# A hybrid state-space and attention layer: other gates in the first stage, keys and queries split two heads at a time, and the time steps projected with the values

## The chip, the cores and the metric

The kernel runs on one core of one Trainium2 chip, as one program with one launch. The core has five engines that run their own instruction streams and wait for one another by semaphores: TensorE (PE in the profile, with PEld for its weight loads), VectorE (DVE), ScalarE (ACT), GpSimd (POOL) and SyncE (SP), which here issues the DMAs. Working data lie in SBUF (128 partitions), matmul results in PSUM, eight banks of 512 fp32 numbers for each partition, and everything else in HBM. The metric is the device time of the program in microseconds, the median of several runs.

## The reference

One layer (D_MODEL 1024) over 512 latent tokens with 256 context tokens ahead of them. Both are normed and modulated; a single input projection feeds everything else:

```python
p_lat = h_lat @ w_in            # columns: z 2048, x/B/C 3072, dt 64, q 1024, k 256, v 256, gates 2048
p_ctx = h_ctx @ w_in
# state-space branch (SSD): 32 heads of 64 in 4 groups, both directions, chunks of 128 tokens
dt = softplus(dt_raw + dt_bias);  la = dt * (-exp(a_log))
y_l = ssd_bidir(xs_l, bm_l, cm_l, dt_l, la_l, state_of_the_context)
ssd_lat = rmsnorm((y_l + d_skip * xs_l) * silu(z), ssd_norm_g)
# attention branch: 16 query heads, 4 key/value heads, width 64, rotary,
# keys: the latent tokens within 128 places, all context tokens, and a sink logit
att_lat = window_ctx_attention(rope(q_l), rope(k_l), v_l, k_c, v_c, sink)
# merge
g = sigmoid(p_lat[..., G0:])
o = (g_ssd * (ssd_lat @ w_o_ssd) + g_att * (att_lat @ w_o_att)) @ w_out
x = x + gt1 * o
x = x + gt2 * conv_ffn(modulate(rmsnorm(x), ...))
```

Three column blocks of `w_in` matter here beside q, k and v: `z`, 16 blocks of 128 columns, which gate the state-space output through a silu; the 2048 columns of the two branch gates, 16 blocks `g`, which pass through a sigmoid; and the 64 columns of `dt`, the time steps of 32 heads in two directions.

## The kernel before

**Numbers.** Everything is fp32. Where a product must be precise, each factor is split into a high part, `hi`, stored as fp32r, and the rest, `lo = x - hi`; the product is then three matmuls, hi·hi, hi·lo and lo·hi. `gemm` (L186) does this for eight blocks of 128 rows of depth. A weight block of 128 x 1024 numbers is loaded by SP into `wraw`, cast to `whi` by ACT (L149) and subtracted to `wlo` by DVE (L150). `run` (L167) takes a list of steps, each with the weight blocks that it needs, and issues the load and split of one block ahead.

**Order.** The first stage's matmuls, and those of the last stages, stand in an order written out by hand. Everywhere else a planner orders the instructions of each engine by what they depend on, so that one engine's order in the program need not be that of the source. Buffers come from pools: a temporary named `ta` has 3 buffers, `tb`, `tc` and `te` 2 each (L113), and a new one waits until an old one's readers, DMAs too, are done. All DMAs stand in SP's one stream.

**First stage (to about 70 us).** While the modulation vectors are made from `w_mod` and the input is normed, the first five branch gates (NG = 5, L294) are projected: `products` (L399) adds up in five PSUM banks `pg`. Since the first rows are used before the norm is known, the shift that modulation adds is brought in at the end as a bias `gb` (L443 to L448). Then a tanh goes to HBM as `ts_d` for each gate (L504 to L507); a sigmoid is kept as tanh(x/2), and the consumer adds 1. Then the context is normed into `hch` and `hcl` (L382 to L387).

**Keys, queries, values.** `k_step` (L592) projects two key heads for latents and context; `rope` (L574) rotates them, and `split_k` (L584) writes each head's hi and lo into the upper and the lower 64 partitions of `khi` and `klo`, by eight ACT and eight DVE instructions. `q_split` (L606) puts one query head's hi into one half of a tile and its lo into the other, so that one matmul with `khi` and one with `klo` give hi and lo at once: two ACT casts and two DVE subtractions on 64 partitions per step. `v_step` (L616) projects the values with tokens on the partitions, 256 columns, two token blocks to a bank.

**Attention (about 100 to 320 us).** Four key heads j and four query blocks b: `block(j, b)` (L650) makes the scores of four heads (one buffer of two banks, L663), takes the minimum on DVE (L675), the exponential on ACT (L679), scales, transposes by TensorE (L697), splits (L700, L701) and multiplies by the values (L702, L703). Between blocks stand projections, `q_step(2)` to `q_step(7)`, `k_step(1)`, and twelve filling steps from the list `fill` (L714): a `z_step` (L515) makes tanh(z/2) on ACT, (tanh + 1)·z on DVE into a `te`, and stores it to `zs_d`; a `g_step` (L527) makes a tanh into a `tb` and stores it to `ts_d` or `ta_d`. The list holds z0 to z15 and then g5 to g15.

**Steps' tables (about 320 to 400 us).** Three more fills (z12 to z14), eight output projections of attention (`oa_step`), and `dt_tables` (L753): a gemm of 64 columns for latents and context, then a chain on ACT and DVE: softplus by a series, with a reciprocal (L769), the decays, and twelve scans along the chunks. `cs_d` goes to HBM.

**The scan (about 400 to 760 us).** For each of four groups: six projections with a short convolution, then four chunks of 128 tokens. `chunk_in` (L1006) loads two 512 KB tables `fb` broadcast from `cs_d` and makes the decay matrix E; `chunk_out` (L1041) multiplies with the forward and the backward state into two parts, each in a `te` (L1050), multiplies E with the inputs into a PSUM bank `yd` (L1054), adds up on POOL (L1059 to L1061) and on DVE (L1062). The next group's projections fill the time; the fourth group has no next one, so it takes fills (L1097): z15, g5, g6 and g7 are each one group's first fill, g8 to g13 fill the fourth group. `gate` (L1066) loads `zs_d` and multiplies.

After it come output projection, merge and the feed-forward part, which the change does not touch.

## Time and profile before

| | |
|---|---|
| median of 3 runs | 1292.92 us (1292.82 to 1294.89) |
| profiled execution | 1291.25 us, of which the span is 1289.5 us |
| granted TensorE clock, mean | 0.998 |
| PE busy | 1260.1 us, 98% of the span, 6482 instructions |
| DVE busy | 899.2 us, 70% |
| ACT busy | 664.8 us, 52% |
| POOL busy | 138.6 us, 11% |
| DMA | 168.66 MB, mean 131 GB/s |

Matmuls overlap one another, so a matmul's recorded length (about 390 ns at 512 columns) is longer than the time that it costs (the distance between two starts). The span runs from the first to the last instruction; an instruction's wait is put down to the one that released it.

### The profile page before, as it was taken

What the parts mean: (1) busy time and instruction counts of PE and PEld (TensorE: products, weight loads), DVE (VectorE), ACT (ScalarE), POOL (GpSimd) and SP (SyncE); (2) the same over time, 40 slices, a digit from 0 to 9 for tenths busy, and PEclk for the clock granted to TensorE, in tenths of its full rate; (3) what the DMA queues carried; (4) which work ended last, traced back from release to release, by engine and by line L of the source; (5) the groups of instructions that cost most, each with busy time, mean ns of one, the idle gap of its engine ahead of it and who ended that gap; (6) DMA issues with size and microseconds to landing.
All of it is one profiled execution on the core that took longest, in us unless ns stands there. A gap on an engine that the chain in (4) does not pass through costs nothing.

```text
span 1289.5 us, 17298 instructions
## 1 busy us (share of the span) xinstructions
PE 1260.1 (98%) x6482; PEld 1025.6 (80%) x6482; DVE 899.2 (70%) x1431; ACT 664.8 (52%) x1230; POOL 138.6 (11%) x113
## 2 busy tenths in 40 slices
PE   7999999999999999999999999999999999999997
PEld 4698777887778878788787777888888888888886
DVE  3867888778495588888888757776677767772323
ACT  3568888767434466475673744223544444442221
POOL 0000000000000043433434440000200000000000
PEclk9999999999999999999999999999999999999999
DMA  8621112222345245454445558867133433333331
GB/s 321 255 94 51 42 58 66 66 74 66 99 127 184 82 117 137 139 134 131 137 140 170 165 192 290 252 221 229 33 115 115 131 114 114 115 107 93 92 101 66
DMA packets 86931, 168.66 MB, mean 131 GB/s; under 512 B 6784, under 2 KB 42112, under 8 KB 86848
## 3 DMA queue, kind: packets, MB, share of 16 engines
q1 hardware_dynamic: 86848, 167.56, 41.5%
q8 instruction: 51, 0.84, 0.3%
q14 instruction: 32, 0.26, 0.1%
HBM read 150.62 MB, written 16.91 MB: 130 GB/s over the span
## 4 chain that ended last, share of the span: by engine, by line
PE 84%; DVE 7%; ACT 5%; issue 2%; DMA 1%; POOL 0%; SPq 0%; DVEq 0%; ACTq 0%; POOLq 0%
PE acc L193 21%; PE acc L192 21%; PE acc L195 21%; PE mis L1054 2%; PE mis L1047 2%; PE score L668 2%; PE pt L697 2%; PE mis L404 2%; PE mis L960 1%; PE po L702 1%; DVE wlo L150 1%; PE mis L888 1%; PE mis L978 1%; PE po L703 1%; PE acc L1196 1%
## 5 line engine op out<-in xcount | busy, mean ns | idle before, releaser
L150 DVE TENSOR_TENSOR wlo<-wraw,whi 128x1024 fp32r<-128x1024 f32 x161 | 203.8, 1266 | 133.0 <-ACT whi L149 131.7
L149 ACT CAST whi<-wraw 128x1024 fp32r<-128x1024 f32 x161 | 166.7, 1036 | 220.7 <-PE acc L193 186.6
L192 PE MATMUL acc<-hlh,whi 128*128 128x512 f32 (+1 forms) x496 | 204.1, 412 | 0.1
L193 PE MATMUL acc<-hll,whi 128*128 128x512 f32 (+1 forms) x496 | 196.1, 395 | 0.0
L195 PE MATMUL acc<-hlh,wlo 128*128 128x512 f32 (+1 forms) x496 | 195.4, 394 | 0.2 <-DVE wlo L150 0.2
L192 PE MATMUL acc<-mh,whi 128*128 128x512 f32 x376 | 146.5, 390 | 0.0
L193 PE MATMUL acc<-ml,whi 128*128 128x512 f32 x376 | 146.4, 389 | 0.0
L195 PE MATMUL acc<-mh,wlo 128*128 128x512 f32 x376 | 146.3, 389 | 0.0
L192 PEld LDWEIGHTS acc<-hlh,whi 128*128 128x128 f32 (+1 forms) x496 | 93.0, 187 | 21.3 <-issue 4.1
L193 PEld LDWEIGHTS acc<-hll,whi 128*128 128x128 f32 (+1 forms) x496 | 93.0, 187 | 19.9 <-issue 4.1
L195 PEld LDWEIGHTS acc<-hlh,wlo 128*128 128x128 f32 (+1 forms) x496 | 92.8, 187 | 19.5 <-issue 1.0
L195 PEld LDWEIGHTS acc<-mh,wlo 128*128 128x128 f32 x376 | 70.6, 188 | 14.8
L192 PEld LDWEIGHTS acc<-mh,whi 128*128 128x128 f32 x376 | 70.6, 188 | 14.7
L193 PEld LDWEIGHTS acc<-ml,whi 128*128 128x128 f32 x376 | 70.6, 188 | 14.6 <-DVE ml L1165 0.2
L962 POOL TENSOR_TENSOR st<-st,eT 128x512 f32<-128x512 f32 x24 | 32.8, 1368 | 410.3 <-ACT st L980 396.7
L860 ACT ACTIVATE ta<-acc,half 128x512 f32<-128x512 f32 (+1 forms) x66 | 46.6, 706 | 41.0 <-PE acc L195 41.0
L245 POOL TENSOR_TENSOR rs<-ms,phalf 128x2 f32<-128x2 f32 (+1 forms) x7 | 6.1, 877 | 548.9 <-DVE ms L244 548.9
L675 DVE CUSTOM_DVE_ANT_0 p<-score,winm,nsink 128x512 f32<-128x512 f32 (+1 forms) x64 | 52.0, 812 | 15.0 <-PE score L668 14.2
L192 PE MATMUL acc<-fh,whi 128*128 128x512 f32 x154 | 60.0, 390 | 0.0
L195 PE MATMUL acc<-fh,wlo 128*128 128x512 f32 x154 | 59.9, 389 | 0.0
L193 PE MATMUL acc<-fl,whi 128*128 128x512 f32 x154 | 59.9, 389 | 0.0
L679 ACT ACTIVATE p<-p,mneg 128x512 f32<-128x512 f32 (+1 forms) x64 | 49.7, 777 | 17.2 <-DVE mneg L675 16.9
(320 smaller groups left out, 2818.8 us busy)
## 6 DMA issues: line engine op xcount, KB each, us to landing
wraw<-wup SPq DMA_DIRECT2D x44, 512.0 KB, 3.6
fb<-cs_d SPq DMA_DIRECT2D x32, 512.0 KB, 6.7
wraw<-wm SPq DMA_DIRECT2D x32, 512.0 KB, 3.6
wraw<-wx SPq DMA_DIRECT2D x24, 512.0 KB, 3.6
wm<-wm SPq DMA_DIRECT2D x16, 512.0 KB, 8.1
wraw<-wz SPq DMA_DIRECT2D x16, 512.0 KB, 3.6
wraw<-wos SPq DMA_DIRECT2D x16, 512.0 KB, 4.6
wraw<-wdn SPq DMA_DIRECT2D x16, 512.0 KB, 3.5
```

The source lines that it names most:

```text
L149: S.copy(hi[:, :n], r[:, :n])
L150: V.tensor_tensor(lo[:, :n], r[:, :n], raw(hi[:, :n]), ALU.subtract)
L192: T.matmul(ps, wh, xh[:, k0 + k, :], start=a, stop=False)
L193: T.matmul(ps, wh, xl[:, k0 + k, :], start=False, stop=False)
L195: T.matmul(ps, wl, xh[:, k0 + k, :], start=False, stop=b)
L404: T.matmul(pg[i], w[a][:, i * P : (i + 1) * P], h[b], start=st and a + b == 0, stop=en and a == 1, skip_group_check=True,)
L668: T.matmul(ps[:, o : o + w], Q[h][:, b * P : (b + 1) * P], k[:, j, z[0] * P : z[0] * P + w], start=v == 0 and o % 512 in (0, P), stop=v == ...
L675: V.tensor_tensor_reduce(p[:, :n], ps[:, o0 : o0 + n], m, op0=ALU.add, op1=ALU.min, scale=1.0, scalar=nsink[:, h : h + 1], accum_out=mn,)
L679: S.activation(p[:, :n], p[:, :n], AF.Exp, bias=mn, scale=-1.0, accum_out=den[:, i : i + 1])
L697: T.transpose(pt[:, i * P : (i + 1) * P], pts[i][:, c * P : (c + 1) * P], ident)
L860: S.activation(o[:, :n], ps[:, :n], AF.Identity, scale=hcol(base_w, stride + i), bias=hcol(base_b, i))
L962: G.tensor_tensor(h8(n), h8(s), bc64(eT[:, z0 : z0 + 8, c]), ALU.mult)
```

## The change

Four things change.

First, the five blocks projected in the first stage are z0 to z4 and no longer g0 to g4. Each now needs a tanh, the value itself with its bias (an Identity on ACT, into a `ta`), a product on DVE, and a store to `zs_d`; the bias is kept twice, halved and whole. The fills follow: attention's twelve are g0 to g2, z5 and g3 to g10; before the steps' tables stand z6 to z8; the groups' first fills are z9, z10, z11 and z12; the fourth group's are z13, z14, z15, g11, g12 and g13.

Second, `q_split` and `split_k` work on 128 partitions, two heads at once: one ACT cast and one DVE subtraction. The halves are then put in their places by DMAs between SBUF tiles, three for a query step and six for a key step (`double_k`).

Third, the steps' 64 columns are appended to the values' 256, so that `v_step` has matmuls of 320 columns, one bank for each of six token blocks. The steps are copied to a `te`, transposed by six TensorE instructions placed in q2's gemm (`steps_turn`, `with_turn`), and stored to `dt_d`.

Fourth, `dt_tables` has no gemm and reads `dt_d`.

```diff
-    src["dt", 0] = wdt, 512
+    for i, n in enumerate((3, 3, 2)):
+        src["v", i] = wv[i, :, : n * 320], n * 320
...
     for i in range(2):
         src["k", i] = wk[i], 1024
-        src["v", i] = wv[i], 1024
...
+    dt_d = dpool.tile([64, L + LC], F32, name="dt_d")
...
-        gb = cpool.tile([P, 8], F32, name="gb")
+        gb = cpool.tile([P, 16], F32, name="gb")
...
-                S.activation(gb[:, v : v + 2 * n - 1 : 2], pbias[:, 256 + 3 * v : 256 + 3 * v + n], AF.Copy, scale=0.5)
+                for c, f in ((0, 0.5), (8, 1.0)):
+                    S.activation(
+                        gb[:, c + v : c + v + 2 * n - 1 : 2], pbias[:, 256 + 3 * v : 256 + 3 * v + n], AF.Copy, scale=f
+                    )
...
             S.activation(t, pg[i], AF.Tanh, scale=0.5, bias=gb[:, i : i + 1])
-            nc.sync.dma_start(ts_d[i], t)
+            z = tmp("ta")
+            S.activation(z, pg[i], AF.Identity, bias=gb[:, 8 + i : 9 + i])
+            V.scalar_tensor_tensor(z, t, 1.0, z, ALU.add, ALU.mult)
+            nc.sync.dma_start(zs_d[i], z)
...
     def split_k(r, t, lo, hi):
-        n = hi - lo
-        for u in range(2):
-            a, j = 64 * u, 2 * t + u
-            for b in (0, 64):
-                S.copy(khi[b : b + 64, j, lo:hi], r[a : a + 64, :n])
-                V.tensor_tensor(klo[b : b + 64, j, lo:hi], r[a : a + 64, :n], raw(khi[b : b + 64, j, lo:hi]), ALU.subtract)
+
+        z = slice(lo, hi)
+        S.copy(khi[:, 2 * t, z], r[:, : hi - lo])
+        V.tensor_tensor(klo[:, 2 * t, z], r[:, : hi - lo], raw(khi[:, 2 * t, z]), ALU.subtract)
+
+    def double_k(t):
+
+        for k in (khi, klo):
+            for a in (64, 0):
+                nc.sync.dma_start(raw(k[a : a + 64, 2 * t + 1, :]), raw(k[64:128, 2 * t, :]))
+            nc.sync.dma_start(raw(k[64:128, 2 * t, :]), raw(k[0:64, 2 * t, :]))
...
             split_k(rc, t, L, 768)
+            double_k(t)
...
     def q_split(ps, t):
+
         r = rope(ps, 1.0)
-        for u in range(2):
-
-            a, b = 64 * u, 64 - 64 * u
-            q = a2p.tile([P, L], F32R, tag="q", name="q", bufs=7)
-            S.copy(q[a : a + 64, :], r[a : a + 64, :])
-            V.tensor_tensor(q[b : b + 64, :], r[a : a + 64, :], raw(q[a : a + 64, :]), ALU.subtract)
-            Q[2 * t + u] = q
+        q = [a2p.tile([P, L], F32R, tag="q", name="q", bufs=7) for _ in range(2)]
+        lo = tmp("tc").bitcast(F32R)
+        S.copy(q[0], r)
+        V.tensor_tensor(lo, r, raw(q[0]), ALU.subtract)
+        for o, i in ((q[1][64:128, :], q[0][64:128, :]), (q[1][0:64, :], lo[64:128, :]), (q[0][64:128, :], lo[0:64, :])):
+            nc.sync.dma_start(raw(o), raw(i))
+        Q.update({2 * t: q[0], 2 * t + 1: q[1]})
 
     def v_step(*w):
 
-        pos = [misb() for _ in range(3)]
+        pos = [misb() for _ in range(5)] + [accb()]
         for k in range(KT):
...
+            wh, wl = (z[:, (k % 3) * 320 : (k % 3 + 1) * 320] for z in w[k // 3])
+            for t, po in enumerate(pos):
+                hh, hl, c0 = (hlh, hll, t) if t < 4 else (hch, hcl, t - 4)
+                c, o = slice(c0 * P, (c0 + 1) * P), po[:, 0:320]
+                T.matmul(o, hh[:, k, c], wh, start=k == 0, stop=False)
+                T.matmul(o, hh[:, k, c], wl, start=False, stop=False)
+                T.matmul(o, hl[:, k, c], wh, start=False, stop=k == KT - 1)
+        steps = tmp("te")
+        for t, po in enumerate(pos):
+            o = po[:, 0:256].rearrange("p (h d) -> p h d", h=4)
+            S.copy(vst[:, t, :, 0:64], o)
+            V.tensor_tensor(vst[:, t, :, 64:128], o, raw(vst[:, t, :, 0:64]), ALU.subtract)
+            S.copy(steps[:, t * 64 : (t + 1) * 64], po[:, 256:320])
+        F["steps"] = steps
+
+    def steps_turn(t0, t1):
+        ps, n = bank("pt"), (t1 - t0) * P
+        for t in range(t0, t1):
+            T.transpose(ps[:64, (t - t0) * P : (t - t0 + 1) * P], F["steps"][:, t * 64 : (t + 1) * 64], ident)
+        o = tmp("tc")
+        S.copy(o[:64, :n], ps[:64, :n])
+        nc.sync.dma_start(dt_d[:, t0 * P : t1 * P], o[:64, :n])
...
-    fill = [z_step(i) for i in range(16)] + [g_step(i) for i in range(NG, 16)]
+    fill = [g_step(i) for i in range(3)] + [z_step(NG)] + [g_step(i) for i in range(3, 11)]
+    fill += [z_step(i) for i in range(NG + 1, 16)] + [g_step(i) for i in range(11, 16)]
...
+    def with_turn(step):
+        def fn(w):
+            BETWEEN.extend([lambda: steps_turn(0, 4), lambda: steps_turn(4, 6)])
+            step[1](w)
...
+    with_[0, 0] = [with_turn(q_step(2))]
...
-    def dt_tables(w):
-        pl, pc = accb(), accb()
-        gemm([(pl[:64, :L], hlh, hll), (pc[:64, :LC], hch, hcl)], w, m=64)
+    def dt_tables():
...
-        S.activation(v[:, :L], pl[:64, :L], AF.Identity, bias=dtv[:, 0:1])
-        S.activation(v[:, L:], pc[:64, :LC], AF.Identity, bias=dtv[:, 0:1])
+        nc.sync.dma_start(v, dt_d)
+        S.activation(v, v, AF.Identity, bias=dtv[:, 0:1])
```

In the host's packing the values' and steps' columns of `w_in` are laid out together in three pieces of 960, 960 and 640 numbers per partition, and the first stage's weights are the first 640 columns of z instead of those of the gates.

More of the change, by code (lines that the diff above doesn't have):

```diff
@@ L59, in tile_hybrid_layer @@
     wq: bass.AP,
-    wdt: bass.AP,
     wx: bass.AP,
@@ L600, in fn @@
             split_k(rc, t, L, 768)
+            double_k(t)
         return [("k", t)], fn
-    Q = {}
+    Q, F = {}, {}
     def q_split(ps, t):
         r = rope(ps, 1.0)
-        for u in range(2):
-            a, b = 64 * u, 64 - 64 * u
-            q = a2p.tile([P, L], F32R, tag="q", name="q", bufs=7)
-            S.copy(q[a : a + 64, :], r[a : a + 64, :])
-            V.tensor_tensor(q[b : b + 64, :], r[a : a + 64, :], raw(q[a : a + 64, :]), ALU.subtract)
-            Q[2 * t + u] = q
+        q = [a2p.tile([P, L], F32R, tag="q", name="q", bufs=7) for _ in range(2)]
[5 more added lines that the diff above has]
+        Q.update({2 * t: q[0], 2 * t + 1: q[1]})
@@ L616, in v_step @@
     def v_step(*w):
-        pos = [misb() for _ in range(3)]
+        pos = [misb() for _ in range(5)] + [accb()]
         for k in range(KT):
-            wh, wl = (z[:, (k % 4) * 256 : (k % 4 + 1) * 256] for z in w[k // 4])
-            for p, po in enumerate(pos):
-                hh, hl, c0 = (hlh, hll, 2 * p) if p < 2 else (hch, hcl, 0)
-                for t in range(2):
-                    c = slice((c0 + t) * P, (c0 + t + 1) * P)
-                    o = po[:, t * 256 : (t + 1) * 256]
-                    T.matmul(o, hh[:, k, c], wh, start=k == 0 and t == 0, stop=False, skip_group_check=True)
-                    T.matmul(o, hh[:, k, c], wl, start=False, stop=False, skip_group_check=True)
-                    T.matmul(o, hl[:, k, c], wh, start=False, stop=k == KT - 1, skip_group_check=True)
@@ L629, in v_step @@
-        for p, po in enumerate(pos):
-            for t in range(2):
-                o = po[:, t * 256 : (t + 1) * 256].rearrange("p (h d) -> p h d", h=4)
-                v = vst[:, 2 * p + t, :, :]
-                S.copy(v[:, :, 0:64], o)
-                V.tensor_tensor(v[:, :, 64:128], o, raw(v[:, :, 0:64]), ALU.subtract)
+            wh, wl = (z[:, (k % 3) * 320 : (k % 3 + 1) * 320] for z in w[k // 3])
[5 more added lines that the diff above has]
+                T.matmul(o, hl[:, k, c], wh, start=False, stop=k == KT - 1)
@@ L645, in tile_hybrid_layer @@
     q_step(0)[1](first["w"][1])
-    run([q_step(1), ([("v", 0), ("v", 1)], v_step)])
+    run([q_step(1), ([("v", i) for i in range(3)], v_step)])
     psum_pools(acc=(2, 1), score=(1, 2), pt=(3, 1), po=(1, 1))
@@ L711, in block @@
             dump("att", att[:, 0, :])
-    F = {}
-    fill = [z_step(i) for i in range(16)] + [g_step(i) for i in range(NG, 16)]
+    fill = [g_step(i) for i in range(3)] + [z_step(NG)] + [g_step(i) for i in range(3, 11)]
+    fill += [z_step(i) for i in range(NG + 1, 16)] + [g_step(i) for i in range(11, 16)]
     n1, n2, n3 = 12, 15, 25
@@ L723, in tile_hybrid_layer @@
     main = []
+    def with_turn(step):
+        def fn(w):
+            BETWEEN.extend([lambda: steps_turn(0, 4), lambda: steps_turn(4, 6)])
+            step[1](w)
+        return step[0], fn
+    with_[0, 0] = [with_turn(q_step(2))]
     for j in range(4):
@@ L849, in tile_hybrid_layer @@
     oas = [oa_step(o) for o in range(8)]
-    run([([], att_split)] + fill[n1:n2] + oas[:1] + [([("dt", 0)], dt_tables)] + oas[1:] + [([], dt_turn)])
+    run([([], att_split)] + fill[n1:n2] + oas[:1] + [([], dt_tables)] + oas[1:] + [([], dt_turn)])
     epool.close()
@@ L1476, in pack @@
     d["wk"] = _cols(w_in, perm(k0, 4))
-    d["wv"] = ca(w_in[:, v0:g0].reshape(2, 4, P, 256).transpose(0, 2, 1, 3).reshape(2, P, 1024))
-    d["w0"] = ca(w_in[:, g0 : g0 + 640].reshape(KT, P, 640))
-    d["wdt"] = ca(w_in[:, dt0:q0].reshape(KT, P, 64).transpose(1, 0, 2).reshape(P, 512))
+    vdt = ca(w_in[:, np.r_[v0:g0, dt0:q0]].reshape(KT, P, 320).transpose(1, 0, 2)).reshape(P, KT * 320)
+    d["wv"] = ca(np.pad(vdt, ((0, 0), (0, 320))).reshape(P, 3, 960).transpose(1, 0, 2))
+    d["w0"] = ca(w_in[:, z0 : z0 + 640].reshape(KT, P, 640))
     d["wx"] = _cols(w_in, A(xbc0, dt0))
```

## The prediction

> **What bounds the kernel now.** I read the page's engine totals and its chain first, then busy time by stretch, then, in each stretch that the change touches, the groups and the timeline.

> The page's head, its engine totals and its chain by engine:

> ```profile
> span 1289.5 us, 17298 instructions
> ...
> PE 1260.1 (98%) x6482; PEld 1025.6 (80%) x6482; DVE 899.2 (70%) x1431; ACT 664.8 (52%) x1230; POOL 138.6 (11%) x113
> ...
> PE 84%; DVE 7%; ACT 5%; issue 2%; DMA 1%; POOL 0%; SPq 0%; DVEq 0%; ACTq 0%; POOLq 0%
> ```

> TensorE is the bound on average. So a change pays in two ways only: matmul time that goes, and places where TensorE stands still. The table by stretch (length, then PE, PEld, DVE, ACT, POOL busy, granted clock, DMA share, GB/s):

> ```profile
> 62.00:104.00 42.00, 42.00 (x269) 38.18 (x268) 26.43 (x47) 27.05 (x48) 0.00 (x0) 1.00 0.31 100
> 104.00:130.00 26.00, 25.89 (x146) 21.27 (x144) 22.32 (x47) 23.84 (x48) 0.00 (x0) 1.00 0.15 49
> 130.00:160.00 30.00, 29.11 (x161) 23.40 (x160) 26.80 (x58) 26.47 (x54) 0.00 (x0) 1.00 0.14 45
> ...
> 690.00:760.00 70.00, 68.77 (x323) 51.61 (x322) 49.96 (x77) 39.15 (x95) 30.42 (x23) 1.00 0.52 167
> ```

> The first attention blocks (104 to 160 us) run with ACT and DVE near 90% busy: there the two are a second bound. Matmuls overlap, so their price is the distance of starts in the timeline: 0.227 us for 512 columns, 0.175 for 384, 0.120 for 256, 0.109 for a 128-column transpose. Distances above that pace add up to some 20 us before 62 us, 8 from 100 to 190, 5 from 190 to 310, and little later. The last stretch belongs to the scan's fourth group, where the two rows below matter (a store of 256 KB, and the same stretch's chain on POOL, DVE and PE):

> ```profile
> L533 SPq DMA_DIRECT2D ta_d<-tb x6: 319/329/383, 710.7 to 758.0; - x6
> ...
> DMA to landing us min/median/max: 2.0/2.2/7.5
> ```

> ```profile
> 715.02 1.00 SPq L1013 DMA_DIRECT2D fb<-cs_d  x2
> 718.13 0.33 SPq L533 DMA_DIRECT2D ta_d<-tb  x1
> ```

> ```profile
> 719.09 2.14 POOL L1060 TENSOR_TENSOR dx<-dx,te 128x512 f32<-128x512 f32 x1 [4.59 <-DVE te L1050]
> 721.31 1.29 POOL L1061 TENSOR_TENSOR dx<-dx,te 128x512 f32<-128x512 f32 x1
> ...
> 722.64 0.69 DVE L1062 TENSOR_TENSOR y<-mis,dx 128x512 f32<-128x512 f32 x1 [1.96 <-POOL dx L1061]
> ...
> 725.79 1.88 PE L1047 MATMUL mis<-st,CT 128*128 128x512 f32 x4
> ```

> The 7.5 is the store of 718.13, right behind two 512 KB loads of fb; it landed at 725.65, the second fb at 725.01. y ends at 723.33 and the next chunk's matmul, which reuses y's PSUM bank, starts at 725.79: 2.5 us of slack.

> **Part by part.** The sum is made against the profiled execution, 1291.25 us (span 1289.5 and 1.75 around it), 1.67 under the median of the runs, 1292.92.

> *TensorE's arithmetic.* The steps' own gemm goes:

> ```profile
> 343.61 0.40 PE L192 MATMUL acc<-hlh,whi 128*64 128x512 f32 x1
> 343.84 0.39 PE L193 MATMUL acc<-hll,whi 128*64 128x512 f32 x1
> 344.07 0.27 PE L192 MATMUL acc<-hch,whi 128*64 128x256 f32 x1
> ```

> 24 matmuls of 512 columns and 24 of 256: 24 x 0.2285 + 24 x 0.1165 = 8.3 us (343.6 to 352). The values' 144 matmuls grow from 256 columns (L626 to L628) to 320. No row has 320; 0.120 and 0.175 are its bounds, the line between them gives 0.147: 144 x 0.027 = +3.9 (0 to 7.9). Six transposes of the steps: 6 x 0.109 = +0.65. Net **-3.8** (-7.6 to +0.3). The weights are as many to split as before.

> *End of the first stage.* Before the context's norm, ACT gets five Identity of some 0.65 (L506's row has 0.689 for a tanh of the size), DVE five gate products of 0.68 (as L522), and two small ACT copies of 0.2 are new. `ta` has three buffers, so the fourth and fifth Identity wait until the stores of z0 and z1 have landed. Today the tanhs already wait here for `ts_d` stores (2.5 us in two waits); the last five hch activations (L386, 0.42 each) now stand behind such a wait, and TensorE needs them for the context half of k0's gemm (67.3 to 70.1). Five of 0.42 late make 2.1; nothing late makes 0. The lighter key split that follows on ACT and DVE helps: **+1.0** (0 to 2.2).

> *From the values into attention.* Before, fifteen matmuls of q2's gemm (3.4 us) stood between the last value matmul and the first score; after, the score of head 0 comes at once. There is one score buffer, so head 1's score waits for head 0's reduction on DVE, and in DVE's order that stands behind the last value copy and subtraction (0.38 + 0.42), and q3's weight split (1.22), then 0.75 itself: 2.77, less the 0.45 of the score: **+2.3** (0 to 2.5). Head 0's ACT work queues behind six added copies of the steps too (no row of 64 columns: 0.20 for 4, 0.38 for 256).

> *Attention, 104 to 310.* Lighter: per q step ACT 2 x 0.62 becomes one of some 0.7 and DVE 2 x 0.686 one of 0.69 (six steps); k1's 4 x 0.62 + 4 x 0.40 on ACT and 4 x 0.69 + 4 x 0.42 on DVE shrink to two instructions each, -3 each; eleven fills change from z to g and lose a DVE product of 0.68 each, -7.5. DVE loses some 15 us, ACT 6 less 2 for the steps' copies. TensorE stands still some 13 us in all here, most of it where both are 90% busy; only what is last in a chain returns: **-3** (-6 to 0). Three transfers per q step and six per k step join SP's queue, the third of each after the first has landed; the weight loads behind them are issued steps ahead and q is needed blocks later, so this costs nothing. If that cover fails it is two quiet landings, 2 x 2.2 = 4.4.

> *Steps' tables, 320 to 390.* Without a gemm the chain starts earlier; on DVE its reciprocal (L769, 4.95 us at 356.12 today) now stands before the split of the first oa weight: TensorE late by some 1.25 (0 to 2.5). Later the wait at 386 for a wlo behind the scans (0.97) shrinks by some 0.75. **+0.5** (-0.75 to 1.7). Reading the steps back adds a DMA to SP's queue, hidden by z fills.

> *Scan, second and third group.* One fill each turns from g to z: a DVE product of 0.68, mostly covered: **+0.3** (0 to 1.4).

> *Scan, fourth group.* Its fills g7 to g13 become z12 to z15 and g11 to g13. A z step takes `te`, of which there are two, and holds it until its store has landed; chunk_out's two parts (L1050) need both. In chunk 1 the second part waits for the landing of z14's store, issued near 717.6 behind the two fb loads, like the 718.13 store. From that landing: 0.68 for the part, 2 x 1.29 on POOL, 0.69 for y, then the matmul: it is late by the landing less 721.8. With the row's 7.5 the store lands near 725.2: +3.4. Chunk 2 repeats it with z15's store, issued near 732.7, 4.5 us behind its fb pair; here the loss is the landing less 735.2. By 7.5 that would be 5.0, held to 3.3 since fb's second load landed 9.5 after its issue and the store just after; by 3.9 (the stretch from 714 to 729 gives two such stores a median of 5.7, so the other took 3.9) it is 1.4. I take 2.4. Queued behind the waiting DVE instruction are coef, the decay products and y. **+5.8** (0 to 6.7).

> [...]

> Sum: -3.8 + 1.0 + 2.3 - 3.0 + 0.5 + 0.3 + 5.8 = **+3.1**, 1294.35 for such an execution, 1296.0 as a median.

> **The rivals.**
> A, the other sign: z14's and z15's stores land as stores usually do here, in 2.2 us. Then the fourth group loses nothing, and the sum is -2.7: 1290.2. It decides below 4.1 us from issue to landing in chunk 1 (2.5 in chunk 2). For it: five of the six `ta_d` stores, at a median of 2.2. Against: the sixth stands where z14's will.
> B, attention returns nothing, because the chains end on the reductions and exponentials, which stay: +6.1, 1299.0. For it: the list of waits from 100 to 330 us names TensorE waits of 3.1 us in all; against: ACT and DVE at 90%, and distances of starts above pace of 13.
> C, no stall anywhere, all cover holds: -3.8 - 3.0 = -6.8, 1286.1. Against: four separate places must all be covered.
> D, the q and k transfers come late once: +3.1 + 4.4 = +7.5, 1300.4. Against: blocks of distance.

> **How the numbers follow.** Forecast 0.50 (own range 1293 to 1300), A 0.26, B 0.12, C 0.08, D 0.04. A measurement of this kernel tells about 0.2%, 2.6 us, from no change. A lies on that border: 0.16 faster, 0.10 within. The forecast's lower end gives 0.08 within, the rest slower. Faster 0.16 + 0.08 = 0.24, same 0.18, slower 0.42 + 0.12 + 0.04 = 0.58. The range 1287.5 to 1302 takes in A, B and D, and leaves out C and tails.

> **What would show it.** In the changed profile: matmuls of 320 columns 0.147 us apart and none of 128*64; ACT waiting for `zs_d` stores near 65 us; a score wait of some 2 us on DVE right after the values; a late wlo behind the reciprocal; L1076 (L1050 before) on DVE waiting for a `zs_d` store twice after 715 us, some 3 us each, and TensorE at the next chunk behind POOL. The prediction is wrong if those stores land within 4 us, or if the stretch from 104 to 310 shortens by more than 6 or not at all.

## The result, and the profile after

The changed kernel takes 1298.43 us (median of 6 runs, 1296.74 to 1299.25) against 1292.87 (6 runs): ratio 1.0042, 95% interval 1.0031 to 1.0052, so 5.6 us slower. Its profiled execution took 1297.72 us. The head of its page, the engine totals and the chain by engine:

```profile
span 1295.9 us, 17285 instructions
...
PE 1260.1 (97%) x6440; PEld 1024.2 (79%) x6440; DVE 887.1 (68%) x1411; ACT 658.5 (51%) x1224; POOL 138.2 (11%) x113
...
PE 81%; DVE 7%; ACT 6%; DMA 3%; issue 2%; POOL 0%; SPq 0%; DVEq 0%; ACTq 0%; POOLq 0%
```

DVE and ACT are 12 and 6 us lighter, and yet the span is 6.4 us longer; the chain has 3% of DMA where it had 1%. By stretch (length, PE, PEld, DVE, ACT, POOL busy, granted clock, DMA share, GB/s):

```profile
62.00:104.00 42.00, 40.80 (x243) 37.45 (x242) 23.34 (x40) 24.08 (x47) 0.00 (x0) 1.00 0.49 144
104.00:130.00 26.00, 24.49 (x133) 19.35 (x132) 20.17 (x44) 21.09 (x44) 0.00 (x0) 1.00 0.24 64
130.00:160.00 30.00, 29.39 (x164) 24.10 (x164) 23.87 (x51) 23.16 (x48) 0.00 (x0) 1.00 0.29 75
...
690.00:760.00 70.00, 65.56 (x281) 48.11 (x280) 48.26 (x75) 36.63 (x89) 27.25 (x22) 0.95 0.50 151
```

ACT and DVE are busy for 77 to 81% now from 104 to 160 us. The last line is the surprise: PE is busy for 3.2 us less, and its granted clock is 0.95 and no longer 1.00.

The two traces are compared at the same matmul in both (starts in us, from the timelines of PE); the last column is what the stage between two rows cost.

| landmark | before | after | later by | stage |
|---|---|---|---|---|
| first matmul of k0 | 61.88 | 61.60 | -0.27 | |
| first of the values | 81.11 | 82.49 | +1.38 | +1.65 |
| last of the values | 98.41 | 103.46 | +5.04 | +3.66 |
| first of the oa steps | 338.17 | 344.25 | +6.09 | +1.04 |
| last of the oa steps | 391.07 | 389.31 | -1.76 | -7.85 |
| first transpose of the third group's gate | 688.94 | 687.31 | -1.63 | +0.13 |
| first of the scan's output projection (os steps) | 768.90 | 774.07 | +5.17 | +6.80 |
| last matmul | 1282.88 | 1289.12 | +6.24 | +1.07 |

Up to the third group's end the kernel is 1.6 us ahead; the fourth group costs 6.8. There, in the timelines of SP, DVE and PE:

```profile
712.41 2.00 SPq L1039 DMA_DIRECT2D fb<-cs_d  x2
...
717.21 0.42 SPq L529 DMA_DIRECT2D zs_d<-te  x1
...
724.47 0.69 DVE L1076 TENSOR_TENSOR te<-mis,TB 128x512 f32<-128x512 f32 x1 [5.25 <-DMA zs_d<-te]
725.08 0.22 DVE L1050 SCALAR_TENSOR_TENSOR coef<-TB,cbd,bcs 128x8 f32<-128x8 f32 x1
725.21 0.72 DVE L1062 COPY_PREDICATED E<-sel,mis 128x512 f32<-128x512 uint8 x1
725.83 1.29 DVE L973 TENSOR_TENSOR xw<-xs,TA 128x512 f32<-128x512 f32 x1
728.28 0.69 DVE L1088 TENSOR_TENSOR y<-mis,dx 128x512 f32<-128x512 f32 x1 [1.15 <-POOL dx L1087]
728.89 0.68 DVE L1064 TENSOR_TENSOR E<-E,mis 128x512 f32<-128x512 f32 x1
...
725.31 1.95 PE L1073 MATMUL mis<-st,CT 128*128 128x512 f32 x4 [1.15 <-DVE coef L1050]
729.71 3.89 PE L1080 MATMUL mis<-xs,E 128*128 128x64 f32 x16 [2.45 <-DVE E L1064]
```

The stores of `zs_d` in the fourth group, by their tile:

```profile
L529 SPq DMA_DIRECT2D zs_d<-te x4: 319/329/424, 699.9 to 732.2; - x4
...
DMA to landing us min/median/max: 2.0/3.4/7.2
```

z14's store, behind two fb loads, is issued at 717.21 and lands 7.2 us later, at 724.4. Until then DVE stands with the second part of the state's product, and behind it in its order stand coef, the predicated copy, y and the decay product E. TensorE waits for coef and for E: 1.15 and 2.45 us. The table of windows shows what follows (before first, then after):

```profile
724.00:730.00 6.00, 5.78 (x26) 3.68 (x25) 4.54 (x8) 4.91 (x12) 1.04 (x1) 1.00 0.75 242
730.00:736.00 6.00, 6.00 (x32) 5.13 (x32) 3.88 (x9) 3.57 (x11) 4.62 (x4) 1.00 0.45 154
```

```profile
724.00:730.00 6.00, 2.41 (x7) 0.99 (x6) 4.38 (x7) 1.80 (x5) 3.81 (x3) 0.96 0.53 165
730.00:736.00 6.00, 6.00 (x21) 4.77 (x21) 3.76 (x6) 4.23 (x10) 0.09 (x1) 0.50 0.43 119
```

From 730 to 736 TensorE is busy all the time at half its clock: the sixteen matmuls of 64 columns are recorded at 3.89 us, where two groups of eight had 1.00 and 1.10 before. The record of the granted clock has 0.50 from 729.55 to 736.38; half of these 6.83 us, an estimated 3.4, is lost beside the 3.6 of standing. z15's store, issued at 732.21, lands within 2.5 us, and nothing waits for it.

From 62 to 104 us the list of PE's waits was empty before. From 60 to 110 us it now has two, the lower one at the end of the first stage, the upper one after the values (us in total, times, longest):

```profile
PE acc L191 <- ACT te L645: 1.3, 1, 1.3
PE acc L191 <- ACT hch L386: 1.2, 1, 1.2
```

### The profile page after: what moved, and what is told of

Read it like the earlier page. It is cut to its first block, busy times and chain, and to the rows that moved or that the text cites. A ratio compares the mean times of both kernels' runs of the same rounds, so it can differ in the third digit from the quotient of the medians.

```text
span 1295.9 us, 17285 instructions
## 1 busy us (share of the span) xinstructions
PE 1260.1 (97%) x6440; PEld 1024.2 (79%) x6440; DVE 887.1 (68%) x1411; ACT 658.5 (51%) x1224; POOL 138.2 (11%) x113
## 4 chain that ended last, share of the span: by engine, by line
PE 81%; DVE 7%; ACT 6%; DMA 3%; issue 2%; POOL 0%; SPq 0%; DVEq 0%; ACTq 0%; POOLq 0%
PE acc L192 20%; PE acc L194 20%; PE acc L191 20%; PE mis L1080 2%; PE score L688 2%; PE mis L1073 2%; PE pt L717 2%; PE mis L986 2%; DVE wlo L149 2%; PE po L722 1%; PE mis L404 1%; PE po L723 1%; PE mis L914 1%; PE mis L1004 1%; ACT ta L583 1%
## 5 line engine op out<-in xcount | busy, mean ns | idle before, releaser
L149 DVE TENSOR_TENSOR wlo<-wraw,whi 128x1024 fp32r<-128x1024 f32 (+1 forms) x161 | 204.3, 1269 | 136.5 <-ACT whi L148 131.0
L148 ACT CAST whi<-wraw 128x1024 fp32r<-128x1024 f32 (+1 forms) x161 | 166.7, 1036 | 223.4 <-PE acc L192 179.6
L191 PE MATMUL acc<-hlh,whi 128*128 128x512 f32 x488 | 202.0, 414 | 1.3 <-ACT te L645 1.3
L192 PE MATMUL acc<-hll,whi 128*128 128x512 f32 x488 | 193.3, 396 | 0.0
L194 PE MATMUL acc<-hlh,wlo 128*128 128x512 f32 x488 | 192.2, 394 | 0.3 <-DVE wlo L149 0.3
L192 PE MATMUL acc<-ml,whi 128*128 128x512 f32 x376 | 146.4, 389 | 0.6 <-DVE ml L1191 0.6
L191 PEld LDWEIGHTS acc<-hlh,whi 128*128 128x128 f32 x488 | 92.0, 189 | 21.4 <-issue 4.1
L192 PEld LDWEIGHTS acc<-hll,whi 128*128 128x128 f32 x488 | 92.1, 189 | 19.5 <-issue 4.1
L194 PEld LDWEIGHTS acc<-hlh,wlo 128*128 128x128 f32 x488 | 91.8, 188 | 19.5 <-issue 1.0
L192 PEld LDWEIGHTS acc<-ml,whi 128*128 128x128 f32 x376 | 70.6, 188 | 15.6 <-DVE ml L1191 0.9
L721 DVE TENSOR_TENSOR ptl<-pt,pth 128x512 fp32r<-128x512 f32 x72 | 47.4, 687 | 23.1 <-ACT pth L720 21.7
```

Source lines behind the costliest of these rows:

```text
L148: S.copy(hi[:, :n], r[:, :n])
L149: V.tensor_tensor(lo[:, :n], r[:, :n], raw(hi[:, :n]), ALU.subtract)
L191: T.matmul(ps, wh, xh[:, k0 + k, :], start=a, stop=False)
L192: T.matmul(ps, wh, xl[:, k0 + k, :], start=False, stop=False)
L194: T.matmul(ps, wl, xh[:, k0 + k, :], start=False, stop=b)
L721: V.tensor_tensor(ptl, pt, raw(pth), ALU.subtract)
```

## Experiments

Four theories: (1) the fourth group's loss is `te` held by z14's store, with the slower clock behind it; (2) attention returned nothing for the lighter ACT and DVE; (3) the steps' part pays 2.3 us; (4) the parts cover for one another. Profiled executions are compared at the landmarks above.

**The order of the fills (e1_swap).**

```diff
-    fill = [g_step(i) for i in range(3)] + [z_step(NG)] + [g_step(i) for i in range(3, 11)]
-    fill += [z_step(i) for i in range(NG + 1, 16)] + [g_step(i) for i in range(11, 16)]
+    fill = [g_step(i) for i in range(3)] + [z_step(NG)] + [z_step(i) for i in range(12, 16)] + [g_step(i) for i in range(7, 11)]
+    fill += [z_step(i) for i in range(NG + 1, 12)] + [g_step(i) for i in range(3, 7)] + [g_step(i) for i in range(11, 16)]
```

> The changed kernel with z12 to z15 exchanged with g3 to g6 in the list of fills: four more z steps in attention, none in the scan's fourth group. Theory 1 (the loss of some 6.9 us in the fourth group is te held by z14's store, and what follows from it): the group loses nothing, 1290 to 1292.5 us, level with the kernel before or a little under. Rival (a z step costs the same wherever it stands, by its DVE product and its store): no change, 1297 to 1299.5.

Measured: 1290.82 us, ratio to before 0.9983 (0.9971 to 0.9995). The fourth group costs 0.4 us less than before instead of 6.8 more. Four z steps more in attention cost nothing there (from the values' end to the last oa step -7.2 us; -6.8 in the changed kernel). Theory 1 holds so far: it is the place of the z step.

**The buffer alone (e2_z_in_ta).**

```diff
-            o = tmp("te")
+            o = tmp("ta" if i > 12 else "te")
```

> The changed kernel with the gate products of z13, z14 and z15 in a ta buffer, which is free in the fourth group, instead of te; same order of fills, same stores at the same place. Theory 1 (the wait is for the buffer): 1290 to 1292.5 us, no wait of DVE for a zs_d store after 700 us, and the granted clock of TensorE stays at 1.00 from 725 to 740. Rival (the stores crowd the fb loads and the decay matrix comes late anyway): 1295 to 1299.

Measured: 1292.05 us, ratio 0.9985 (0.9975 to 0.9995). The stores are where they were, and the slowest of them takes 7.4 us to land, where z14's took 7.2; but nobody waits for it, and the clock stays up:

```profile
724.00:730.00 6.00, 6.00 (x32) 4.16 (x31) 5.53 (x8) 5.11 (x13) 0.39 (x1) 1.00 0.76 204
730.00:736.00 6.00, 6.00 (x32) 5.08 (x31) 3.89 (x9) 3.80 (x13) 4.61 (x4) 1.00 0.84 270
```

So it was the wait for the buffer, and neither the product nor the traffic. The fourth group now costs 0.1 us less than before.

**The old splits in the changed kernel (e3_old_qk).** `q_split` and `split_k` are those of before; `double_k` and its transfers go.

> The changed kernel with the old splits of queries and keys (two heads one after the other, no transfers). Theory 2 (attention's chains end on reductions and exponentials, so the lighter ACT and DVE returned nothing): 1297 to 1299.5 us. Rival (the prediction's 3 us are in there, covered by something else that grew): 1300.5 to 1302.

Measured: 1305.18 us, ratio 1.0089 (1.0072 to 1.0106), 6.7 us over the changed kernel and beyond both expectations. Theory 2 in that form falls: in this kernel the new splits are worth more than the 3 us predicted. The trace has TensorE waiting 0.62 and 1.74 us for two reductions of block (0, 3) at 157 to 160 us, the clock at 0.50 for 3.4 us after it, and at 380 us 2.27 for a wlo, with no fall after it.

**The old steps in the changed kernel (e4_old_steps).** `v_step` with 256 columns, the gemm in `dt_tables`, no `steps_turn`.

> The changed kernel with the old values step of 256 columns and the old gemm of the steps in their own stage. Theory 3 (the step pays 8.3 us and costs 3.9 of wider matmuls, 0.65 of transposes, 1.4 of a wait for the steps' copies): 2.3 us slower than the changed kernel, 1300 to 1301.5. Rival (the copies and the late weight split eat all of it): 1297 to 1299.

Measured: 1300.02 us, ratio 1.0051 (1.0036 to 1.0066), 1.6 us over the changed kernel, where theory 3 says 2.3. The two intervals overlap (1.0042, 1.0031 to 1.0052, for the changed kernel), so this run supports theory 3 no more than it refutes it.

**Each part alone on the kernel before (e5_qk_only, e6_steps_only, e7_z_only).** The first has only the new splits, the second only the wider values step and its transposes, the third only the other gates and the new list.

> The kernel before with the new splits of queries and keys alone. Prediction's term (3 us in attention): 1288.5 to 1291.5 us. Theory 2 (attention gives nothing back): 1292 to 1294. Rival from the run that took the splits out of the changed kernel, which lost 6.7 us (the splits are worth that wherever they are): 1285.5 to 1288.

> The kernel before with the steps projected along with the values alone. Theory 3 (8.3 us of gemm less 3.9 of wider matmuls, 0.65 of transposes, 1.4 for the steps' copies): 1290 to 1291.5 us. Rival (the old splits keep ACT and DVE so busy that the copies and the late weight split eat it): 1292.5 to 1295.

> The kernel before with the other gates in the first stage and the new list of fills alone. Theory 1 (te held by z14's store in the fourth group costs 3.9 us of standing and 3 of a slower TensorE clock; the first stage 1.4): 1299.5 to 1302 us, granted clock below 0.9 in the stretch from 725 to 745. Rival (the fourth group's loss needs the other parts' timing): 1293 to 1297.

Measured: 1296.72 us (ratio 1.0027, 1.0016 to 1.0037), 1297.93 (1.0037, 1.0024 to 1.0050) and 1303.94 (1.0087, 1.0073 to 1.0101). The first is above the prediction's term and theory 2, the second above both of its expectations; the third is over its range in the direction of theory 1. Less work on ACT and DVE made the kernel slower; the trace of the splits alone shows a wait in block (3, 3) that has grown from 1.16 us to 4.08, PE first, then DVE ahead of it:

```profile
318.22 2.23 PE L704 MATMUL pt<-ident,p 128*128 128x128 f32 x8 [4.08 <-DVE p L697]
...
315.66 1.22 DVE L150 TENSOR_TENSOR wlo<-wraw,whi 128x1024 fp32r<-128x1024 f32 x1
316.80 0.16 DVE L691 TENSOR_TENSOR es<-es,den 128x4 f32<-128x4 f32 x1
316.87 0.68 DVE L522 SCALAR_TENSOR_TENSOR te<-tb,acc 128x512 f32<-128x512 f32 x1
317.47 0.17 DVE L692 RECIPROCAL es<-es 128x4 f32<-128x4 f32 x1
```

In the planner's order a weight split and the last z fill's product come ahead of the reciprocal on which the block's transposes hang, and on TensorE a single matmul of the fill is left to cover them, where the changed kernel has eleven and waits for 0.78 us only. The clock falls again:

```profile
314.00:318.00 4.00, 0.14 (x1) 0.00 (x0) 3.92 (x10) 3.02 (x9) 0.00 (x0) 0.79 0.04 4
318.00:324.00 6.00, 5.78 (x22) 4.30 (x23) 2.43 (x5) 3.06 (x6) 0.00 (x0) 0.57 0.25 85
```

With the steps alone, the old key splits fall between the reductions of block (0, 3), DVE first, then PE:

```profile
150.92 2.83 DVE L590 TENSOR_TENSOR klo<-tb,khi 64x512 fp32r<-64x512 f32 x4
153.79 0.75 DVE L682 CUSTOM_DVE_ANT_0 p<-score,winm,nsink 128x512 f32<-128x512 f32 x1
154.47 0.08 DVE L682 DVE_READ_ACCUMULATOR2_ANT mneg<- 128x1 f32 x1
154.47 1.76 DVE L590 TENSOR_TENSOR klo<-tc,khi 64x256 fp32r<-64x256 f32 x4
...
154.61 0.39 PE L675 MATMUL score<-khi,q 128*128 128x256 f32 x1 [0.63 <-DVE mneg L682]
...
157.08 0.58 PE L675 MATMUL score<-khi,q 128*128 128x256 f32 x1 [1.73 <-DVE mneg L682]
```

In the changed kernel the same two subtractions take 0.69 and 0.42 us, and no wait is listed there. The third kernel repeats the fourth group's loss, larger: waits of 3.21, 0.95 and 0.86 us and two falls of the clock, 9.7 us in all.

**Two parts together (e11_qk_steps), and with another order of copies (e12_acc_steps).** The first has the splits and the steps, with the old gates and fills; the second also takes the accumulator bank of the values first.

```diff
-        pos = [misb() for _ in range(5)] + [accb()]
+        pos = [accb()] + [misb() for _ in range(5)]
```

> The changed kernel with the old gates in the first stage and the old list of fills: the new splits and the projected steps together, on the kernel before. Theory 4 (the two parts cover for each other: alone they were 3.3 and 4.5 us slower, because each leaves one place where TensorE stands long enough for its clock to halve): 1289 to 1291.5 us, no fall of the clock between 100 and 760 us. Rival (each part costs what it cost alone): 1299 to 1302.

> As the run before it, with the values' accumulator bank first, so that its copies are first. Theory (the 1.4 us at the steps' copies is that bank's wait): 1.4 us under the run before it, 1287.5 to 1290, level with the best so far. Rival (the planner moves another wait in): the same time as the run before it.

Measured: 1298.79 us (ratio 1.0036, 1.0021 to 1.0052) and 1297.91 (1.0031, 1.0020 to 1.0042). Theory 4 falls in this form: the time does not come back. Together the two parts cost 5.3 us, though, and their separate costs add up to 7.8. Both kernels have the wait of block (3, 3), 4.07 and 4.08 us, and 2.28 at an oa weight. The wait after the values, 1.59 us in the first, is gone in the second. It was that of a score for a reduction, not of an accumulator bank, so the theory of the second run had its cause wrong. The time is 0.9 us less, which the two intervals don't tell from nothing.

With these the eight combinations of the three parts are all measured. From the last values matmul to the last oa step, in profiled executions, against before, with the 8.3 us of the steps' gemm taken out of the count where it is gone:

| new list and gates | new splits | new steps | us |
|---|---|---|---|
| no | no | no | 0 |
| no | yes | no | +3.4 |
| no | no | yes | +7.9 |
| yes | no | no | +0.7 |
| no | yes | yes | +9.0 |
| yes | no | yes | +6.9 |
| yes | yes | no | -1.4 |
| yes | yes | yes | +1.5 |

Each row is one profiled execution. Where other runs have the same code up to there, they agree within 0.2 us: e9_hold3 and e10_hold5 below with before, e2_z_in_ta with the changed kernel.

No part has a price of its own here. The splits alone cost 3.4 and, on the list and the steps, save 5.4; the list alone costs 0.7 and, on the other two, saves 7.5. The rows with a loss of 3 us or more have long waits of TensorE in the planner's order, and falls of its clock behind some of them; that these make up the whole of each row was not measured.

**The two remaining waits (e8_norm_first).** The exchange of e1_swap, the accumulator first, and the context's norm ahead of the gates:

```diff
-        for i in range(NG):
-            t = tmp("tb")
...
         for j in range(KT):
             norm(j, 1, xc_, r["c"], hch, hcl)
+        for i in range(NG):
+            t = tmp("tb")
...
```

> The changed kernel with three edits: z12 to z15 exchanged with g3 to g6 as before; the values' bank that is an accumulator comes first, so that its copies are first; the context's norm stands ahead of the first stage's gates in the program. Theory (first stage's 1.4 and the 1.4 at the steps' copies are both waits for ACT's order): 1288 to 1290 us. Rival (the two waits only move to the gates' banks and to the other steps' copies): 1290 to 1292.5.

Measured: 1289.57 us, ratio to before 0.9973 (0.9962 to 0.9983): faster than both kernels. Its interval overlaps that of e1_swap, so what the two further edits are worth is read from the stretches alone. In its profiled execution the stretch from k0 to the values costs 0.0 and no longer 1.65, and from the values' end to the last oa step it gains 8.8 us instead of 6.8. It is 5.2 us ahead of the kernel before at the scan's output projection and gives 3.7 of that back later, 1.5 within that projection, where its clock falls for 3.4 us near 770, and 1.9 in the projections behind it.

**The clock alone (e9_hold3, e10_hold5).** The kernel before, with idle POOL work between the sums of the fourth group's first chunk, 3 or 5 times:

```diff
             G.tensor_tensor(dx, dx, parts[1], ALU.add)
+            for _ in range(3 if (g, c) == (3, 0) else 0):
+                G.tensor_tensor(dx.rearrange("p (a b) -> p a b", b=P), dx.rearrange("p (a b) -> p a b", b=P), ones.unsqueeze(1).to_broadcast([P, 4, P]), ALU.mult)
```

> The kernel before with three idle POOL multiplications by one, some 1.3 us each, between the two sums of the first chunk of the scan's fourth group: y is 3.9 us later, of which 2.5 are slack. Theory (a halved TensorE clock follows when TensorE stands for some 3 to 4 us in a short time, whatever it waits for): one wait of 1 to 1.6 us, granted clock stays at 1.00. Rival (any wait there is followed by it): clock 0.5 for some us.

> As the run with three, with five: y is 6.5 us later, TensorE stands for some 4 us, in one piece or two. Theory (halved clock after 3 to 4 us of standing): granted clock 0.5 for 4 to 7 us afterwards, loss 4 us of standing and 2 to 3.5 more. Rival (the slow clock belongs to the store and the loads at work in the changed kernel): clock 1.00, loss 4 us alone.

Measured, one execution each: 1295.59 and 1303.18 us, against 1294.26 for the kernel before beside them. PE's waits and the windows behind them, with three first, then with five:

```profile
729.01 1.08 PE L1054 MATMUL mis<-xs,E 128*128 128x64 f32 x8 [1.52 <-DVE E L1038]
...
730.94 1.10 PE L1054 MATMUL mis<-xs,E 128*128 128x64 f32 x8 [0.85 <-DVE E L1038]
```

```profile
730.00:736.00 6.00, 5.15 (x26) 4.05 (x26) 3.92 (x7) 5.26 (x15) 2.22 (x2) 1.00 0.50 146
```

```profile
733.14 1.94 PE L1054 MATMUL mis<-xs,E 128*128 128x64 f32 x8 [4.56 <-DVE E L1038]
```

```profile
730.00:736.00 6.00, 2.86 (x10) 2.37 (x11) 4.29 (x7) 2.29 (x6) 2.64 (x3) 0.70 0.16 55
736.00:742.00 6.00, 6.00 (x26) 4.92 (x25) 3.71 (x7) 2.95 (x10) 4.54 (x4) 0.74 0.33 108
```

2.4 us of standing cost 2.5 at the next landmark; 4.6 us cost 7.0. No z store is in the fourth group of these kernels, and e2_z_in_ta had the stores with the clock at 1.00, so here the slower clock follows from standing, not from the transfers.

## Why the prediction was right, and where it was not

The time, 1298.43 against 1296.0, and the sign were right, by terms of which some were wrong. The forecast was +3.1 us and the change cost 5.6. That the time came so near is in part luck: a term of 2.4 that didn't come was replaced by 3.4 that no term had. Of the signs that were to show it, the score's wait was not there, and of the two waits for a store only one. z15's store landed within the 4 us that the prediction named as a sign of being wrong.

*TensorE's arithmetic.* Right to some 0.3 us: 320 columns are 0.147 us apart, the values cost +3.66 (predicted 3.9), and the oa stage with the gemm gone -7.85 (predicted -8.3 and +0.5).

*End of the first stage.* +1.65 for 1.0, inside its bounds, and by the mechanism told: ACT waited 1.53 us for a z store, five hch activations stood behind it, and TensorE waited 1.20 for the first of them. With the norm first the cost is gone.

*From the values into attention.* Wrong in its place: head 1's score was not late. The wait, 1.27 us instead of 2.3, is that of q2's gemm for an accumulator bank whose steps ACT had not yet copied out, because the sixth bank of `v_step` is an accumulator and is copied last, here behind a weight cast. The predicted wait does exist with the old gates and list: e6_steps_only and e11_qk_steps have a score waiting 1.59 us for the reduction. The prediction named the added copies only as something head 0's work would queue behind.

*Attention.* From the values' end to the first oa step it is +1.04, of which 0.65 are the transposes and 1.43 that late start: so the lighter engines returned about 1.0 us, and not 3, and the stretch as a whole did not shorten. The step that failed is "only what is last in a chain returns", taken as a share of TensorE's standing: the table of eight shows that the return depends on the planner's order, and is anything from a loss of 3.4 to a gain of 5.4 for the same work taken away, the splits'. Rival B was close on this term, and its time, 1299.0, is nearer to the measured one than the forecast.

*Steps' tables.* Right: the reciprocal is ahead of the split, TensorE waits 0.46 and 0.64 us at 345 and 347, and the later wait at a wlo is gone.

*Scan, fourth group.* +6.80 for 5.8, but not as built. The first chunk is right: issue at 717.21 for 717.6, landing in 7.2 us for 7.5, 3.6 us of standing for 3.4. y's bank was not what TensorE met: it waited 1.15 us for what stands directly behind the late part on DVE, and 2.45 for the decay product that is queued behind y. The second chunk's 2.4 didn't come: the z store was issued 5.3 us after the second fb load instead of some 4.5, that load landed 5.8 us after its issue instead of 9.5, and the store landed in 2.5 us, the bound below which the prediction has no loss. In its place came 6.8 us at half the clock, 3.4 us lost, which no term had. In the run with five, 4.6 us of standing were followed by such a clock, in the run with three 2.4 were not. The length of standing alone doesn't tell: with the steps alone, 0.63 and 1.73 us were followed by a clock of 0.56 from 156 to 162.

*Rival A* fell on the store's landing: 7.2 us, near the 7.5 of the row behind two fb loads, and the rival needed a landing below 4.1. z15's landed in 2.5. Rival D didn't occur: no wait for a q or k transfer is in the list. Rival C's -6.8 is near what e8_norm_first shows at the output projection, -5.2.

*Not foreseen:* +1.07 after the scan. On DVE the modulation step waits for its weights, and the merge of the last output block is queued behind it, before first, then after:

```profile
863.93 0.75 DVE L552 SCALAR_TENSOR_TENSOR tm<-wraw,csil,tm 128x512 f32<-128x512 f32 x1 [0.90 <-DMA wraw<-wm]
```

```profile
870.07 0.75 DVE L558 SCALAR_TENSOR_TENSOR tm<-wraw,csil,tm 128x512 f32<-128x512 f32 x1 [2.29 <-DMA wraw<-wm]
```

Why that load came later stays open.

## What to carry to other kernels

A buffer that is held by a store had the store's landing time as its price here: 7.2 us for z14's, issued 3.2 us after the second of two 512 KB loads, and 2.5 for z15's, issued 5.3 us after the second of the next two. Put such steps where no large load has just been issued, or give them a buffer that nobody else needs (e2_z_in_ta: 7.4 us to land, and no wait for it). Where a planner orders the engines, the price of an edit is not its own: read the new order for the one place where a fill no longer covers a chain. And behind TensorE's standing of 3.6 us (the changed kernel), 4.1 (e5_qk_only, e11_qk_steps, e12_acc_steps) and 4.6 (e10_hold5) it lost an estimated 1.7 to 3.4 us more to the slow clock, half of the time that it then ran at 0.50; of the waits of 2.3 to 2.4 us some cost only themselves and some, by the same estimate, 1.7 to 3.4 more, so the longest wait is the first to break.

## What the runs showed of the hardware

| run | TensorE waits, us | idle share of the step or steps | clock in the next step |
|---|---|---|---|
| e9_hold3 | 1.52, 0.85 | 0.45, 0.25 | 1.00 |
| e3_old_qk, at 380 us | 2.27 | 0.33, 0.34 | 1.00 |
| e6_steps_only, at 155 us | 0.63, 1.73 | 0.59 | 0.50 |
| e3_old_qk, at 158 us | 0.62, 1.74 | 0.63 | 0.50 |
| e11_qk_steps, at 372 us | 2.28 | 0.67 | 0.50 |
| the changed kernel, at 728 us | 2.45 | 0.67 | 0.50 |

From 62 to 760 us, in all 14 traces, the 13 falls followed a step idle for 0.53 or more, and no step at the full clock idle for 0.48 or less was followed by one. Elsewhere this doesn't hold: falls before 46 us and from 765 to 790 followed steps idle for 0.18 to 0.54, and why stays open. The clock also falls in stretches where the kernels have the same code: in the first 46 us it stayed at 1.00 in the profiled executions of before and after, and fell in others:

```profile
26.00:36.00 10.00, 9.38 (x78) 6.06 (x76) 4.93 (x12) 3.86 (x7) 1.02 (x1) 1.00 0.79 257
```

```profile
26.00:36.00 10.00, 9.71 (x70) 6.44 (x69) 4.11 (x9) 2.64 (x6) 1.01 (x1) 0.83 0.97 341
```

The first is of before, the second of e8_norm_first, whose first matmul of k0 is no later for it (61.85 against 61.88). Between e9_hold3 and e10_hold5, with the same code up to the fourth group, it is: 61.55 without a fall, 62.87 with one from 39.4 to 42.9 us, which may be some of the spread between runs of one kernel.
